# First half of the output weights: from one block at a border to side work of the attention

## The chip, the cores and the metric

One core of one Trainium2 chip runs the whole program. The metric is the device time of one execution in microseconds (us). The engines are named as in the profile: PE (TensorE, matmuls; PEld is its weight load), DVE (VectorE), ACT (ScalarE), POOL (GpSimd) and SP (SyncE, which here only issues transfers). Each engine takes its instructions in the order in which they were written into its queue, and an instruction that has to wait holds up all behind it on that engine. That holds for SP and POOL too when they issue DMAs.

## The reference, cut to what matters

An encoder layer over 2304 tokens (2048 of one sequence, 256 of another), width 1024. The change lies in how one operand of the second line is brought in:

```
n = rms_norm(x) ; [u|q|k|v] = n @ w_in
mix = concat(rms_norm(S5(u)) * ssm_out_g, rms_norm(dilated_attention(q,k,v)) * attn_out_g)
x   = x + mix @ w_out                       # w_out is 1024 x 1024
x   = x + (silu(g) * up) @ w_down , [g|up] = conv3(rms_norm(x) @ w_up)
```

Rows 0 to 511 of `w_out` multiply the S5 half of `mix` (the "a" half of the weights), rows 512 to 1023 the attention half (the "b" half). All of it is float32, and every product is made of three matmuls of split operands: each operand is a rounded part (hi) and the rest (lo), and hi\*hi + hi\*lo + lo\*hi is summed.

## The kernel before

The program runs in stages: input projection, S5 with the q/k projection, attention (with the GLU of the S5 half beside it), output projection with the second norm, up projection with the convolution, down projection. This document is about the attention and the start of the output projection.

**The attention** (from L1062 on) goes over 8 heads, two to a pair `hp`. A head has three patterns and a part for the short sequence, in 21 groups. A group is a chain over three engines: matmuls into `s` (L967, L968), a DVE reduction with the bias `bt` into `sb` (L973), an exponential on ACT (L974), transposes on PE into `pt` (L153), a copy of `pt` to `pb` (L957 on ACT or L958 on DVE; in pair 0 all on DVE), and matmuls with the values `v` into `po` (L1005, L1134). Each head has one small transpose into `pts` after its first pattern and one product `pop` near its end; both serve here as marks. At a head's second pattern POOL issues the loads of the next head's `qs`, `kh` and `kl` (L939), and SP loads the values `v` of the next pair when the old ones are free (L914 to L927). `weights` and `join` mix the three patterns of a head: SP stores and fetches small factors (`w_d`, `wb`), POOL multiplies `ot` by them, and the result goes to `ob_d`.

**Side work** fills PE beside the heads. `side_work` (L1057) says at which of the groups one step of a generator is taken. In pair 0 that is `glu`. From head 2 on it is `project_all` (L881), the projection of the S5 half: for each of 16 token tiles it loads `pat` and `pxt`, splits `pat` into `pah` (hi on ACT, L867; lo on POOL, L868), makes 24 matmuls into `ppa` (L156 to L158, 128x512) and adds the result to `pxt` on DVE (L879). A tile takes 4 steps. 48 of 120 groups take one, that is 8 a head and 12 tiles in all; the 4 tiles left are drained after the last head, before the two "early" tiles of the short sequence, whose matmuls also write `ppa`.

**The weights** are brought in by `out_weight` (L851), 8 pieces of 128x512: a load on SP (L163) into `wsoa` or `wsob`, hi on ACT (L168, into `ohia` or `ohib`) and lo on DVE (L169, into `oloa` or `olob`). The a half is called at the border between pair 0 and pair 1 (L1176), all 8 pieces in a row, with one staging buffer, since the pool `woa` has one buffer of each name. The b half is called after the attention, with two.

**What sets the order.** The lines above are not the order in the queues. A scheduler that comes with the language simulates the program and writes each engine's queue, taking earlier written work first among what it thinks is ready. So the loads of the a half, written at the border after head 1, stand in the queues from the end of the GLU on, inside head 0.

Of the kernel before, what the change touches and what calls it, by code (L numbers as in the profile page):

```python
# [10 lines left out]
F32 = mybir.dt.float32  # L11
# [3 lines left out]
AF = mybir.ActivationFunctionType  # L15
ALU = mybir.AluOpType
# [4 lines left out]
P = 128  # L21
# [51 lines left out]
def tile_encoder(ctx: ExitStack, tc: tile.TileContext, x_prompt, x_sample, norm_mix_g, w_in,  # L73
# [3 lines left out]
    nc = tc.nc  # L77
    V = nc.vector
    A = nc.scalar
# [3 lines left out]
    def mkpool(name, bufs, space=None, side=None):  # L83
        kw = {}
        if space is not None:
            kw["space"] = space
        if side is not None:
            kw["side"] = side
        return tc.tile_pool(name=name, bufs=bufs, reuse_waits="tile", **kw)
# [71 lines left out]
    def split_weight(wpool, spool, src, k0, c0, w, g, hi, lo, nm):  # L161
        s = spool.tile([P, w], F32, name="ws" + nm, tag="wstage")
        ld = nc.sync.dma_start(out=s, in_=src[k0:k0 + P, c0:c0 + w])  # L163
        if g is None:
            A.activation(hi, s, AF.Copy)
            V.tensor_tensor(lo, s, hi.bitcast(F32), ALU.subtract)
        else:
            A.activation(hi, s, AF.Copy, scale=g)  # L168
            V.scalar_tensor_tensor(lo, s, g, hi.bitcast(F32), ALU.mult, ALU.subtract)  # L169
        return ld  # L170
# [342 lines left out]
    def drain(gen, n=None):  # L513
        k = 0
        for _ in gen:
            k += 1
            if n is not None and k >= n:
                return
# [329 lines left out]
    GROUPS = [[16, 17, 0, 1, 2, 3], list(range(4, 10)), list(range(10, 16))]  # L848
    NLATE = 2

    def out_weight(wp, wst, k0, nm):  # L851
        hi = wp.tile([P, 4, D], F32R, name="ohi" + nm)
        lo = wp.tile([P, 4, D], F32R, name="olo" + nm)
        for k in range(4):
            for h in range(2):
                hs_ = slice(h * 512, (h + 1) * 512)
                split_weight(wp, wst, w_out[0], (k0 + k) * P, h * 512, 512, gains[:, 8 + k0 + k:9 + k0 + k],
                             hi[:, k, hs_], lo[:, k, hs_], f"o{nm}{k}{h}")
        return hi, lo

    def project_a(t, w, ap_, xt, psm, tag, behind=(None,)):

# [7 lines left out]
        for h in range(2):  # L870
# [7 lines left out]
                    yield  # L878
            V.scalar_tensor_tensor(xt[:, hs_], ps, rab[:, t:t + 1], xt[:, hs_], ALU.mult, ALU.add)  # L879

    def project_all(w, ap_, xp, psm):  # L881
        for t in TOKS[NLATE:]:
            xt = xp.tile([P, D], F32, name=f"pxt{t}", tag="xt")
            yield from project_a(t, w, ap_, xt, psm, "g", last_copy)
            nc.sync.dma_start(out=x1_d[t * P:(t + 1) * P, :], in_=xt)
            yield
# [62 lines left out]
    with pa:  # L949
# [107 lines left out]
        def side_work(hp, n):  # L1057

            if hp == 0:
                return n % 6 == 0  # L1060
            n -= 40
            return n * 48 // 120 != (n + 1) * 48 // 120  # L1062

        for hp in range(4):
            cs = slice(hp * P, (hp + 1) * P)
# [105 lines left out]
            if hp == 0:  # L1171
                drain(gen)
                pg.close()
                woa = right.enter_context(mkpool(name="woa", bufs=1, side="right"))
                apa = right.enter_context(mkpool(name="apa", bufs=2, side="right"))
                wa = out_weight(woa, woa, 0, "a")  # L1176
                gen = project_all(wa, apa, right.enter_context(mkpool(name="xpa", bufs=2, side="right")), ps_g)


    pu = ctx.enter_context(ExitStack())  # L1180
# [3 lines left out]
    wsum = pu.enter_context(mkpool(name="wsum", bufs=3))  # L1184
    pd = ctx.enter_context(ExitStack())
    wp = pd.enter_context(mkpool(name="wo", bufs=1))
    wst = pd.enter_context(mkpool(name="wsto", bufs=2))
    ap_ = pd.enter_context(mkpool(name="apd", bufs=2))
    xp = pd.enter_context(mkpool(name="xpd", bufs=3))
    sm = pd.enter_context(mkpool(name="smd", bufs=3))  # L1190
# [60 lines left out]
            downw[divmod(e + i, KF)] = hl[:, :, i]  # L1251

    downw = {}
    ohi, olo = out_weight(wp, wst, 4, "b")
    drain(gen)
    pgs.close()
    psm = pu.enter_context(mkpool(name="psmD", bufs=4, space=PSUM))
    pst = pu.enter_context(mkpool(name="pstD", bufs=3, space=PSUM))
# [252 lines left out]
```

## Time and profile before

| | |
|---|---|
| median of 3 runs | 2878.91 us (2878.47 to 2884.9) |
| the profiled execution | 2880.48 us, its span 2878.7 us |
| busy share of the span | PE 95%, PEld 85%, DVE 65%, ACT 46%, POOL 22% |
| mean granted TensorE clock | 0.974 |
| attention, from the first `pts` to the last `pop` | 711.4 to 1159.7 us |
| splits of the a half on ACT | 8, from 717.8 to 807.1 us |
| splits of the b half on ACT | 8, from 1163.1 to 1200.3 us |

The table is read from the page and from the views of single tiles. The busy shares are means over stages that differ; what a change in one stage is worth is read in that stage. The granted clock is 1.0 at 2.4 GHz and 0.5 at 1.2 GHz, so a stretch with 0.9 spent a fifth of its time at the lower level.

### The profile page before, as it was taken

To read this page: it belongs to the slowest core of one execution; us is meant where nothing else is said; L and a number is where in the kernel's file an instruction comes from. 1 tells how busy PE (TensorE), PEld (TensorE's weight loads), DVE (VectorE), ACT (ScalarE), POOL (GpSimd) and SP (SyncE) were. 2 spreads that over 40 slices of the span, in tenths; PEclk is the share of its full clock that TensorE was granted. 3 is DMA by queue.
4 is the path that set the end of the run, shared out by engine and by line. 5 is a ranking of instruction groups with operands and counts; after the bars stand their busy time and mean duration, and the time that the engine had idled before them with its cause. 6 is when DMAs were issued, how large, how long until landed. Compare 5 with 4: busy or idle time off the path is not lost. (4 is left out here: it accounts for less than half of the span.)

```text
span 2878.7 us, 43567 instructions
## 1 busy us (share of the span) xinstructions
PE 2744.7 (95%) x15488; PEld 2458.3 (85%) x15488; DVE 1860.5 (65%) x4274; ACT 1322.6 (46%) x2723; POOL 646.9 (22%) x1120
## 2 busy tenths in 40 slices
PE   7998889998989999888999999999999989999999
PEld 7887667788878888777999999999999978888887
DVE  5776899977745445587989997778877742223221
ACT  3354454545566666244555565556655531112110
POOL 0587533312343432220111011113100000000000
PEclk9999999999999999999999999999999999999999
DMA  7574888777788685657555555544544462224221
GB/s 215 167 249 130 252 229 233 197 188 173 148 174 193 155 195 125 227 177 228 170 174 174 192 188 156 156 156 136 167 152 152 131 182 86 74 85 142 86 84 47
DMA packets 483991, 471.04 MB, mean 164 GB/s; under 512 B 87985, under 2 KB 406077, under 8 KB 480701
## 3 DMA queue, kind: packets, MB, share of 16 engines
q1 hardware_dynamic: 465084, 425.25, 50.2%
q0 software_dynamic: 18688, 43.01, 6.4%
q8 instruction: 122, 2.00, 0.3%
q14 instruction: 97, 0.79, 0.1%
HBM read 308.63 MB, written 159.55 MB: 163 GB/s over the span
## 5 line engine op out<-in xcount | busy, mean ns | idle before, releaser
L156 PE MATMUL pf<-dw,ah 128*128 128x512 f32 x792 | 309.6, 392 | 4.9 <-ACT dw L1194 4.9
L157 PE MATMUL pf<-dw,ah 128*128 128x512 f32 x792 | 309.7, 392 | 1.7 <-DVE dw L1195 1.7
L158 PE MATMUL pf<-dw,ah 128*128 128x512 f32 x792 | 309.3, 391 | 0.0
L1479 DVE TENSOR_TENSOR acc<-pf,acc 128x512 f32<-128x512 f32 x72 | 49.7, 691 | 383.0 <-PE pf L158 383.0
L1465 ACT ACTIVATE ah<-at 128x512 fp32r<-128x512 f32 x72 | 53.1, 784 | 410.4 <-PE pf L158 410.4
L974 ACT ACTIVATE sb<-sb,st 128x256 f32<-128x256 f32 (+2 forms) x384 | 172.4, 451 | 32.9 <-DVE st L973 29.0
L1194 ACT ACTIVATE uw<-su 128x1024 fp32r<-128x1024 f32 x132 | 139.5, 1058 | 97.2 <-PE pu_5p L1378 5.6
L156 PEld LDWEIGHTS pf<-dw,ah 128*128 128x128 f32 x792 | 149.9, 189 | 37.7 <-ACT dw L1194 6.4
L157 PEld LDWEIGHTS pf<-dw,ah 128*128 128x128 f32 x792 | 149.6, 189 | 34.3 <-DVE dw L1195 3.0
L158 PEld LDWEIGHTS pf<-dw,ah 128*128 128x128 f32 x792 | 149.7, 189 | 30.7
L1195 DVE TENSOR_TENSOR uw<-su,uw 128x1024 fp32r<-128x1024 f32 x132 | 160.8, 1219 | 17.4 <-ACT uw L1194 17.3
L1422 POOL COPY r<-edge 128x2 f32<-128x2 f32 x88 | 58.3, 663 | 481.6 <-DVE h L1433 465.2
L1430 DVE SCALAR_TENSOR_TENSOR h<-r,convp,h 128x255 f32<-128x255 f32 (+3 forms) x176 | 139.8, 815 | 38.8 <-ACT h L1427 37.7
L1427 ACT ACTIVATE h<-r,convp 128x767 f32<-128x767 f32 (+2 forms) x132 | 135.5, 1028 | 63.8 <-DVE r L1414 61.2
L967 PE MATMUL s<-kh,qs 128*128 128x256 f32 (+2 forms) x384 | 151.4, 403 | 1.0 <-DVE dn L973 0.7
L1424 POOL COPY edge<-r 128x2 f32<-128x2 f32 x88 | 68.9, 783 | 368.3 <-DVE r L1414 232.6
L958 DVE COPY pb<-pt 64x128 f32<-64x128 f32 (+2 forms) x150 | 74.3, 505 | 108.1 <-PE pt L153 107.5
L1433 DVE SCALAR_TENSOR_TENSOR h<-r,convp,h 128x768 f32<-128x768 f32 (+2 forms) x176 | 140.7, 814 | 1.4
L968 PE MATMUL s<-kl,qs 128*128 128x256 f32 (+2 forms) x384 | 138.0, 369 | 0.0
L973 DVE CUSTOM_DVE_ANT_0 sb<-s,bt 128x256 f32<-128x256 f32 (+2 forms) x384 | 121.0, 357 | 13.9 <-PE pt L153 11.6
L500 POOL TENSOR_TENSOR q<-ph,phs 128x64 f32<-128x64 f32 (+6 forms) x352 | 119.4, 374 | 2.1
L153 PE MATMUL pt<-ctab,sb 128*128 128x128 f32 (+1 forms) x640 | 103.2, 284 | 8.2 <-ACT sb L974 5.9
(934 smaller groups left out, 7648.2 us busy)
## 6 DMA issues: line engine op xcount, KB each, us to landing
us<-in_w_up_dram SPq DMA_DIRECT2D x88, 512.0 KB
su<-ws_d SPq DMA_DIRECT2D x88, 512.0 KB
at<-act_d SPq DMA_DIRECT2D x36, 704.0 KB
ws_d<-su SPq DMA_DIRECT2D x44, 512.0 KB
qk_d<-qt SPq DMA_DIRECT2D x72, 256.0 KB
wb<-w_d SPq DMA_DIRECT2D x32, 384.0 KB
us<-in_w_up_dram SPq DMA_DIRECT2D x44, 256.0 KB
ds<-in_w_down_dram SPq DMA_DIRECT2D x44, 256.0 KB
```

What stands on the lines that cost most here:

```text
L156: mm = T.matmul(ps, lhi, rhi, start=first, stop=False)
L157: T.matmul(ps, lhi, rlo, start=False, stop=False)
L158: T.matmul(ps, llo, rhi, start=False, stop=last)
L967: T.matmul(ps[:, c:c + n], qs[:, q], khi[:, keys], start=True, stop=False)
L968: T.matmul(ps[:, c:c + n], qs[:, q], klo[:, keys], start=False, stop=True)
L973: V.tensor_tensor_reduce(sb[:, c:c + n], ps[:, c:c + n], bias, 1.0, 3e38, ALU.add, ALU.min, mn)
L974: A.activation(sb[:, c:c + n], sb[:, c:c + n], AF.Exp, bias=mn, scale=-1.0, accum_out=den)
L1194: A.activation(dst[:, 0], src, AF.Copy)
L1195: V.tensor_tensor(dst[:, 1], src, dst[:, 0].bitcast(F32), ALU.subtract)
L1427: A.activation(h[:, a:b], r[:, a:b], AF.Identity, bias=cw[:, 3], scale=cw[:, 1])
L1430: V.scalar_tensor_tensor(h[:, c0:c1], r[:, c0 - 1:c1 - 1], cw[:, 0], h[:, c0:c1], ALU.mult, ALU.add)
L1433: V.scalar_tensor_tensor(h[:, c0:c1], r[:, c0 + 1:c1 + 1], cw[:, 2], h[:, c0:c1], ALU.mult, ALU.add)
```

## The change

The a half becomes the first part of the generator `project_all`: three pieces are loaded ahead, and each step loads one more and splits one. It has a pool of its own, `wsa`, with four staging buffers. The b half uses the same code with four buffers in place of two, and is drained at once where it stood. Side steps are 55 of 120 groups in place of 48, of which the first 8 go to the weights.

```diff
-    def out_weight(wp, wst, k0, nm):
+    def out_weight(wp, wst, k0, nm, out):
         hi = wp.tile([P, 4, D], F32R, name="ohi" + nm)
         lo = wp.tile([P, 4, D], F32R, name="olo" + nm)
-        for k in range(4):
-            for h in range(2):
-                hs_ = slice(h * 512, (h + 1) * 512)
-                split_weight(wp, wst, w_out[0], (k0 + k) * P, h * 512, 512, gains[:, 8 + k0 + k:9 + k0 + k],
-                             hi[:, k, hs_], lo[:, k, hs_], f"o{nm}{k}{h}")
-        return hi, lo
+        def load(i):
+            k, c = divmod(i, 2)
+            t = wst.tile([P, 512], F32, name=f"wso{nm}{i}", tag="wstage")
+            nc.sync.dma_start(out=t, in_=w_out[0, (k0 + k) * P:(k0 + k + 1) * P, c * 512:(c + 1) * 512])
+            return t
+        stage = [load(i) for i in range(3)]
+        for i in range(8):
+            if i + 3 < 8:
+                stage.append(load(i + 3))
+            yield
+            k, c = divmod(i, 2)
+            cs, g = slice(c * 512, (c + 1) * 512), gains[:, 8 + k0 + k:9 + k0 + k]
+            A.activation(hi[:, k, cs], stage[i], AF.Copy, scale=g)
+            V.scalar_tensor_tensor(lo[:, k, cs], stage[i], g, hi[:, k, cs].bitcast(F32), ALU.mult, ALU.subtract)
+        out.append((hi, lo))
...
     def project_all(w, ap_, xp, psm):
+        yield from out_weight(*w, 0, "a", outw)
+        w = outw[0]
         for t in TOKS[NLATE:]:
...
-            return n * 48 // 120 != (n + 1) * 48 // 120
+            return n * 55 // 120 != (n + 1) * 55 // 120
...
-                wa = out_weight(woa, woa, 0, "a")
-                gen = project_all(wa, apa, right.enter_context(mkpool(name="xpa", bufs=2, side="right")), ps_g)
+                wsa = right.enter_context(mkpool(name="wsa", bufs=4, side="right"))
+                gen = project_all((woa, wsa), apa, right.enter_context(mkpool(name="xpa", bufs=2, side="right")), ps_g)
...
-    wst = pd.enter_context(mkpool(name="wsto", bufs=2))
+    wst = pd.enter_context(mkpool(name="wsto", bufs=4))
...
-    ohi, olo = out_weight(wp, wst, 4, "b")
+    drain(out_weight(wp, wst, 4, "b", outw))
+    ohi, olo = outw[1]
     drain(gen)
+    wa = outw[0]
```

The orders of the two programs are the same up to head 0's `pts` and again from the first products of the up projection on. Line numbers of the changed program differ: its load is L859, its hi L869, its lo L870; lines behind stand 12 to 18 higher.

**SP, from the end of the GLU to the values of pair 1.** Before, in head 0 (`at_d` is the last store of the GLU; `st_d`, `r`, `w_d` and `wb` belong to the mix of head 0):

```order
L1152 DMA st_d_120<-s_8404 32x128
L833 DMA at_d<-ga_9084 128x4x256
L163 DMA wsoa_9671<-in_w_out_dram 128x512
L163 DMA wsoa_9675<-in_w_out_dram 128x512
L1155 DMA st_d_120<-st_8417 128x4x4 x2
L1012 DMA r_8903<-st_d_120 128x4x16
L163 DMA wsoa_9679<-in_w_out_dram 128x512
L163 DMA wsoa_9683<-in_w_out_dram 128x512
L163 DMA wsoa_9687<-in_w_out_dram 128x512
L1168 DMA ob_d<-obp_8949 64x128 x2
L1029 DMA w_d_128<-w_8906 128x3x16
L1038 DMA wb_8953<-w_d_128 64x3x512 x2
```

Now, in head 1 (the first five rows stand before too, without the pieces behind them):

```order
L1168 DMA st_d_121<-s_9242 32x128
L930 DMA v_9675<-v_d 128x15x128
L1064 DMA ob_d<-ot_8061 64x512 x2
L931 DMA v_9675<-v_d 64x128
L932 DMA v_9675<-v_d 64x128
L859 DMA wsoa_9750<-in_w_out_dram 128x512
L859 DMA wsoa_9752<-in_w_out_dram 128x512
L859 DMA wsoa_9754<-in_w_out_dram 128x512
L859 DMA wsoa_9756<-in_w_out_dram 128x512
L877 DMA pat_10207<-at_d 128x4x128
L881 DMA pxt_10206<-in_x_sample_dram 128x1024
```

Before, five pieces were issued in head 0 and the sixth just ahead of the values of pair 1; the seventh and eighth came behind. Now all eight stand behind those values, four of them at once and ahead of the first `pat`.

**ACT, in the third pattern of head 1.** Before (the seventh piece is `wsoa_9695`):

```order
L974 ACTIVATE sb_9423,st_9255<-sb_9423,st_9255 128x192
L168 ACTIVATE ohia<-wsoa_9695,gains 128x512
L974 ACTIVATE sb_9455,st_9452<-sb_9455,st_9452 128x128 x4
L974 ACTIVATE sb_9480,st_9452<-sb_9480,st_9452 128x128 x4
L974 ACTIVATE sb_9523,st_9452<-sb_9523,st_9452 128x128 x3
L867 ACTIVATE pah_9782<-pat_9780 128x512
```

Now (the first piece is `wsoa_9750`):

```order
L990 ACTIVATE sb_9423,st_9255<-sb_9423,st_9255 128x192
L990 ACTIVATE sb_9455,st_9452<-sb_9455,st_9452 128x128 x3
L869 ACTIVATE ohia<-wsoa_9750,gains 128x512
L990 ACTIVATE sb_9455,st_9452<-sb_9455,st_9452 128x128
L990 ACTIVATE sb_9480,st_9452<-sb_9480,st_9452 128x128 x4
L869 ACTIVATE ohia<-wsoa_9752,gains 128x512
L869 ACTIVATE ohia<-wsoa_9754,gains 128x512
L990 ACTIVATE sb_9523,st_9452<-sb_9523,st_9452 128x128 x4
L990 ACTIVATE sb_9548,st_9452<-sb_9548,st_9452 128x128
L1158 ACTIVATE ot_9254<-po_9359 128x2x256
L990 ACTIVATE sb_9548,st_9452<-sb_9548,st_9452 128x128 x3
L869 ACTIVATE ohia<-wsoa_9756,gains 128x512
```

In the place of one split (the seventh) four stand there (the first to the fourth), and the first `pah` comes right behind the last row. The other four splits stand in head 2, in its first pattern and behind it.

**SP, at the end of the attention.** Before, around the first pieces of the b half (`ot_14025` is the load of the first tile of the output projection, `pat_13946` that of the first early tile, `wb` the factors of the last head):

```order
L1029 DMA w_d_135<-w_13653 128x3x16
L163 DMA wsob_13758<-in_w_out_dram 128x512
L1168 DMA ob_d<-obp_13696 64x128 x2
L163 DMA wsob_13762<-in_w_out_dram 128x512
L885 DMA x_d<-pxt_13790 128x1024
L865 DMA pat_13946<-at_d 128x4x128
L1038 DMA wb_13700<-w_d_135 64x3x512 x2
L1296 DMA ot_14025<-ob_d 128x4x128
```

Now:

```order
L1054 DMA wb_13705<-w_d_135 64x3x512 x2
L877 DMA pat_13949<-at_d 128x4x128
L859 DMA wsob_13753<-in_w_out_dram 128x512
L859 DMA wsob_13755<-in_w_out_dram 128x512
L859 DMA wsob_13757<-in_w_out_dram 128x512
L859 DMA wsob_13759<-in_w_out_dram 128x512
L881 DMA pxt_13865<-in_x_sample_dram 128x1024
L877 DMA pat_13984<-at_d 128x4x128
L1314 DMA ot_14029<-ob_d 128x4x128
```

The second pair of `wb` loads, which needs the buffer that POOL's first three products free, now stands ahead of the first early `pat`; before, it stood behind the loads of both early tiles. The load of `ot` has moved behind four pieces.

**PE, the `ppa` matmuls**, counted in the two orders between the marks:

| stretch | before | now |
|---|---|---|
| head 0 `pts` to head 1 `pts` | 0 | 0 |
| head 1 to head 2 | 18 | 0 |
| head 2 to head 3 | 48 | 24 |
| head 3 to head 4 | 48 | 60 |
| heads 4, 5 and 6, each to the next | 48 | 54 |
| head 7 `pts` to its `pop` | 52 | 54 |
| from there to the output projection | 122 | 132 |

In the last stretch the first matmul of an early tile stands behind 51 others before, and behind 72 now.

## Rows read from the trace of the kernel before

**Rows 1.** Busy time by stretch: us, engines' busy us and counts, clock, DMA share, GB/s.
```profile
711.40:764.40 53.00, 51.22 (x401) 44.13 (x400) 38.91 (x163) 32.05 (x109) 12.11 (x13) 0.90 0.60 126
764.40:826.60 62.20, 53.28 (x409) 45.00 (x408) 36.90 (x157) 36.20 (x127) 23.48 (x23) 0.95 0.89 189
826.60:882.80 56.20, 54.51 (x430) 46.43 (x429) 28.67 (x135) 36.69 (x127) 29.50 (x28) 1.00 0.81 166
...
997.50:1055.30 57.80, 57.80 (x436) 49.20 (x434) 28.34 (x137) 36.50 (x129) 23.27 (x23) 0.94 0.79 196
...
1159.70:1200.20 40.50, 31.81 (x134) 25.47 (x133) 18.95 (x23) 9.85 (x16) 15.73 (x13) 0.91 0.80 258
1200.20:1335.00 134.80, 122.00 (x591) 101.78 (x592) 110.95 (x453) 62.94 (x88) 28.91 (x34) 0.94 0.58 191
```

**Rows 2.** Busy time of `ppa` alone, two stretches: us, PE, PEld, DVE, clock.
```profile
1172.00:1182.30 10.30, 5.78 (x14) 4.42 (x15) 1.41 (x2) 0.68 0.70 235
1182.30:1196.00 13.70, 13.66 (x60) 10.96 (x58) 1.40 (x2) 0.99 0.78 251
```

**Rows 3.** The tile `wsoa`: what its splits waited for (us, times).
```profile
  DMA wsoa<-in_w_out_dram: 12.1, 5
```

**Rows 4.** ACT in time, heads 0 and 1: start, us, instruction, [idle before, releaser].
```profile
717.82 0.71 ACT L168 ACTIVATE ohia<-wsoa,gains 128x512 fp32r<-128x512 f32 x1
...
734.39 0.72 ACT L168 ACTIVATE ohia<-wsoa,gains 128x512 fp32r<-128x512 f32 x1 [4.62 <-DMA wsoa<-in_w_out_dram]
...
765.12 0.72 ACT L168 ACTIVATE ohia<-wsoa,gains 128x512 fp32r<-128x512 f32 x1 [2.44 <-DMA wsoa<-in_w_out_dram]
...
786.60 0.72 ACT L168 ACTIVATE ohia<-wsoa,gains 128x512 fp32r<-128x512 f32 x1 [4.36 <-DMA wsoa<-in_w_out_dram]
...
795.95 0.63 ACT L867 ACTIVATE pah<-pat 128x512 fp32r<-128x512 f32 x1 [4.39 <-DMA pat<-at_d]
```

**Rows 5.** PE in time, heads 0 and 1: its two longest waits for ACT.
```profile
735.55 0.47 PE L153 MATMUL pt<-ctab,sb 128*128 128x128 f32 x1 [1.34 <-ACT sb L974]
...
797.01 0.48 PE L153 MATMUL pt<-ctab,sb 128*128 128x128 f32 x1 [4.60 <-ACT sb L974]
```

**Rows 6.** SP in time: when the loads were issued.
```profile
713.60 6.31 SPq L163 DMA_DIRECT2D wsoa<-in_w_out_dram  x2
...
767.16 0.38 SPq L914 DMA_DIRECT2D v<-v_d  x1
...
770.76 0.83 SPq L163 DMA_DIRECT2D wsoa<-in_w_out_dram  x1
...
773.64 0.59 SPq L865 DMA_DIRECT2D pat<-at_d  x1
```

**Rows 7.** DMA issues from 700 to 830: count, KB each, median us to landing.
```profile
kl<-qk_d POOLq DMA_DIRECT2D x4, 576.0 KB, 19.3
```

**Rows 8.** Busy time by stretch, as in rows 1: head 0's wait and the loads' stretch.
```profile
730.00:740.00 10.00, 8.66 (x57) 6.90 (x56) 5.45 (x29) 5.41 (x22) 0.00 (x0) 0.77 0.74 113
740.00:760.00 20.00, 19.56 (x184) 16.85 (x184) 18.48 (x68) 14.95 (x49) 7.04 (x6) 0.86 0.18 45
...
780.00:800.00 20.00, 15.22 (x127) 12.97 (x125) 9.15 (x47) 10.43 (x41) 7.19 (x8) 0.92 1.25 233
```

**Rows 9.** PE in time behind the last `pop`: its two waits.
```profile
1176.52 0.79 PE L156 MATMUL ppa<-ohia,pah 128*128 128x512 f32 x1 [4.62 <-ACT pah L867]
...
1200.15 0.80 PE L156 MATMUL pw<-ohib,mix 128*128 128x512 f32 x1 [4.08 <-DVE x L879]
```

**Rows 10.** ACT in time there.
```profile
1174.40 0.63 ACT L1302 ACTIVATE mix<-ot 128x512 fp32r<-128x512 f32 x1 [7.21 <-DMA ot<-ob_d]
...
1175.85 0.61 ACT L867 ACTIVATE pah<-pat 128x512 fp32r<-128x512 f32 x1
```

**Rows 11.** SP in time there.
```profile
1163.57 1.69 SPq L1038 DMA_DIRECT2D wb<-w_d  x2
1165.36 1.95 SPq L1296 DMA_DIRECT2D ot<-ob_d  x2
...
1192.64 0.43 SPq L869 DMA_DIRECT2D x<-in_x_prompt_dram  x1
```

More of the change, by code (lines that the diff above doesn't have):

```diff
@@ L879, in project_a @@
             V.scalar_tensor_tensor(xt[:, hs_], ps, rab[:, t:t + 1], xt[:, hs_], ALU.mult, ALU.add)
+    outw = []
     def project_all(w, ap_, xp, psm):
+        yield from out_weight(*w, 0, "a", outw)
+        w = outw[0]
         for t in TOKS[NLATE:]:
```

## The prediction

> **What bounds the kernel now.** I read the busy shares first, then busy time by stretch between the marks `pts`, then each engine in time where a stretch is longer than its PE work, then the issues on SP and the latency of the loads.
>
> In the attention PE is the bound wherever it has side work: a stretch with 48 `ppa` matmuls is 57.8 us long with 57.8 us of PE work [rows 1]. Side work at full clock costs 13.66 us for 60 matmuls, 0.228 us each [rows 2]; the 48 are 10.9 us, so the heads' own part of such a stretch is 57.8 - 10.9 = 46.9 us.
>
> The two stretches that the a half touches stand apart. Head 0's has 53.0 us with 51.22 of PE and clock 0.90; the next, with only 18 `ppa` matmuls, has 62.2 us with 53.28 of PE [rows 1]. Less work takes longer there. ACT shows why: its splits wait 12.1 us for `wsoa`, in 5 times [rows 3], 4.62 us in head 0, 2.44 and 4.36 in head 1, and then 4.39 more for the first `pat` [rows 4]. An exponential stands behind each, and PE waits for it 1.34 and 4.60 us [rows 5].
>
> How long a piece takes depends on what else is being loaded. The first, issued at 713.60 [rows 6], is split at 717.82 [rows 4]: 4.2 us. The seventh, issued at 770.76 behind `v`, is split at 786.60: 15.8 us. `pat`, issued at 773.64, is used at 795.95: 22.3 us. In that time POOL's loads for the next head (`kl`, 576 KB, 19.3 us to landing [rows 7]) and SP's `v` share the DMA engines: 780 to 800 us moves 233 GB/s with PE busy 15.22 of 20 us, while 740 to 760 moves 45 [rows 8]. The DMA engines lie nearly idle just where the old pieces stood, and are full where the new ones go. The Trainium skill ("DMA: Bandwidth & Descriptors", Issuing engines are not separate DMA queues) says that transfers started by SP and by GpSimd run on the same 16 DMA engines and interleave. By that rule more pieces in this stretch delay each other and `pat`; the trace agrees, 15.8 us for a piece here against 4.2 in head 0.
>
> **Part by part.** Copies and splits are as many as before (16 loads, 16 hi, 16 lo), and the `ppa` matmuls are 432 in both. What changes is where they stand.
>
> *Head 0* loses five loads, and the splits with them. What can be won is between the 1.34 us that PE waited visibly [rows 5] and the 4.62 us that ACT stood [rows 4]. But 740 to 760 us, where no piece is waited for, has PE at 19.56 of 20 us at clock 0.86, with DVE at 18.48 of 20 [rows 8]: in pair 0 DVE also makes all copies, so it stays close to the bound. I take **-2**.
>
> *The border and head 1* (the 62.2 us stretch). The wait of 2.44 at 765 us goes, since no piece stands there. The 18 `ppa` matmuls leave: 18 x 0.228 = 4.1 us. Against that, four splits stand in the third pattern where one stood. The seventh piece was issued at 770.76 and waited for until 786.60; the first new one goes out in `pat`'s old place, 773.64 [rows 6]. With the same latency of 15.8 us it lands at 789.4. ACT came to its split at 786.60 - 4.36 = 782.2 [rows 4], so it waits 7.2 us in place of 4.4, with at most five rows of exponentials in between to soften it. Three more pieces follow in SP's queue, 0.75 MB, at 233 GB/s 3.4 us; the three splits behind use that up while ACT works. `pat` comes behind them, but its `pah` is now wanted only behind four splits and at head 2, so its 4.39 us goes. What bounds this: below, both waits of the third pattern go, 2.44 + 4.36 = 6.8 us won; above, the splits wait as long as `pat` did (22.3 us from 773.64 is 795.9, 13.7 us behind 782.2) with no help from the wait that goes, 13.7 - 4.4 = 9.3, some 8 with the exponentials ahead. I take **+3** before the side work that leaves, since the seventh piece is the nearest row and half of what ACT loses reached PE before.
>
> *Side work put elsewhere.* The two stretches of heads 1 and 2 lose 18 + 24 = 42 `ppa` matmuls, 9.6 us. They come back in full in stretches that PE fills (12, 6, 6 and 6 more in heads 3 to 6, 2 in head 7, 10 behind it: 42), +9.6. The question is what heads 1 and 2 give up for it. A stretch cannot shrink under its slowest other engine: head 0's with no `ppa` is 53.0 us, not 46.9 [rows 1], and the one with 24 left would be 46.9 + 24 x 0.228 = 52.4 at best against 56.2 now, a gain of 3.8 at most, and with four splits more on ACT and DVE I take 2.4. Head 1's, 62.2 long, should give back its 4.1 in full, as PE was held up there by ACT and not by its own work. Together 6.5 given up, 9.6 paid: **+3**. Bounds: 0 where all of it shrinks, +5.5 where only head 1's 4.1 does.
>
> *The tail.* Between the last `pop` and the output projection PE is busy 31.81 of 40.5 us [rows 1]. Two waits make 8.7 us: 4.62 for the first early tile's `pah` and 4.08 for `x` [rows 9]. The first is a queue matter: ACT stands 7.21 us for `ot` at 1174.40, and `pah` follows at 1175.85 [rows 10]. Now 72 - 51 = 21 more matmuls stand ahead of that early tile, 21 x 0.228 = 4.8 us of cover, just the size of the wait. But SP is held by the second `wb`, which waits for three POOL products, and now stands ahead of `pat`, four pieces, `pxt` and `ot`; before, `wb` and `ot` were issued at 1163.57 and 1165.36 [rows 11] with `pat` already out. The 4 pieces are 1 MB, 3.9 us at that stretch's 258 GB/s [rows 1]. The last `x` was issued at 1192.64 [rows 11] and with deeper staging goes out sooner, so part of the 4.08 can go too. The clock of 0.68 behind the first wait [rows 2] rises or falls with it. Ends: -8.7 and, with both waits paid a second time, +8. I take **0**: the cover and the added queue are of a size.
>
> *The four buffers of the b half* let pieces start two earlier. The splits there end at 1200 with PE waiting for `x`, not for a piece, so nothing is won apart from the tail's term. The stages before head 0 and behind the first up products have the same order: 0.
>
> **The sum.** -2 + 3 + 3 + 0 = +4 on the profiled 2880.48: 2884.5. The median of the runs stands 1.6 below the profiled execution, so the forecast is **2883**. That the loads are "three ahead" is no gain by itself: in the queues the old pieces stood in the quiet head 0, and the new ones come later, not earlier.
>
> **The rivals.**
>
> *A, faster: the loads land before they are wanted.* Four pieces go out together ahead of the first split. If ACT reaches the first split later than the queue tells, or the first piece takes nearer 10 us than 15.8, no split waits. Then head 0 gives 2 to 4.6, the third pattern 2.44 + 4.36, the tail 4.08, less the side work's 3: -9.9 to -12.5, and up to 1.6 more with the clock of 780 to 800 (0.92 [rows 8], so 8% of 20 us lost to the lower level): -10 to -14 on the median, 2865 to 2869. For it: 780 to 800 has 4.8 us of idle PE to give. Against: the latency row. The Trainium skill ("DMA: Bandwidth & Descriptors", Rules for kernel authors) says to issue a DMA early, compute, and wait on its semaphore late; by that rule this is the outcome, if early meant the place in the queue. The trace speaks against it here, with 773.6 for the first issue in place of 713.6. Chance 0.23.
>
> *B, slower: the first piece is stuck among the loads of head 2 and the values.* Place: ACT, third pattern of head 1. The first piece takes as long as `kl` or `pat` (19.3 to 22.3 us), ACT's four splits take the exponentials behind them along, PE idles and its clock falls to the lower level for some us. Price: 9 us of wait over the old one, 3 to 5 for the pieces behind it and `pat`, 2 for the clock (1.6 were lost there before), with the side work's 3 and less head 0's 2: +15 to +17, 2894 to 2896. It decides when the first piece lands 10 us or more behind ACT's arrival. For it: DMA share 1.25 in that stretch [rows 8]. Against: POOL's loads were issued earlier and are partly through by 789. Chance 0.17.
>
> *C, slower by little: the tail loses.* SP, held by `wb`, issues the early `pat` and `ot` late; PE waits 5 us more for `pah`, with the rest as forecast: +9, 2888. It decides when the early `pat` is issued later than some 1170, since 72 matmuls (16.4 us) cover a latency of that length behind the last `pop` at 1159.7. Chance 0.13.
>
> **How the numbers follow.** The forecast has the 0.47 that are left. 0.3% of 2878.9 is 8.6 us, about what a measurement of this kernel can tell from no change. Faster by that (under 2870.3): nearly all of A, 0.22, and 0.01 of the forecast's lower tail. Slower (over 2887.5): B's 0.17, half of C, 0.06, and 0.05 of the forecast, together 0.28. Within: the rest, 0.49. The range reaches from inside A to just over B, 2866 to 2897; what is left out is the case where all of head 0's, head 1's and the tail's gains come at once, and the one where B and C do.
>
> **What would show it.** Head 0's stretch near 51 us with no wait for a piece on ACT. A wait of about 7 us on ACT ahead of the first `wsoa` split in head 1 and no long one ahead of the three behind it; none there means A, over 10 means B. `pts` marks some 61 us apart from head 1 to head 2, 54 from 2 to 3, 60.5 from 3 to 4, 59 after that. No PE wait of 4 us ahead of the early tile; one of 8 or more with a late `pat` means C. I am wrong in the mechanism if the pieces land in under 10 us in that stretch, or if heads 1 and 2 shrink by the full 9.6 us of the work that leaves them.

## The result and the profile after

The changed kernel takes 2906.47 us (median of 3, 2904.01 to 2911.17) against 2878.91: the ratio is 1.0089, 95% interval 1.0069 to 1.0108. It is slower, beyond the upper end of the forecast range (2897). Its profiled execution takes 2904.01 us with a span of 2902.2, 23.5 us over the span before.

Busy time by stretch of the changed kernel, columns as in [rows 1]; the first five stretches run from one `pts` to the next (heads 0, 1, 2, 3 and 5), the last is the tail from the last `pop` to the output projection:

```profile
709.69:759.25 49.56, 47.65 (x401) 41.30 (x399) 35.70 (x161) 30.15 (x108) 15.94 (x16) 0.97 0.51 103
759.25:818.06 58.81, 51.84 (x394) 44.61 (x393) 35.62 (x150) 38.23 (x128) 19.43 (x21) 0.85 0.87 213
818.06:889.57 71.51, 54.03 (x402) 45.59 (x401) 27.81 (x137) 35.30 (x122) 31.20 (x30) 0.83 0.55 108
889.57:952.05 62.48, 59.78 (x447) 50.83 (x446) 28.41 (x139) 38.57 (x132) 20.98 (x22) 0.97 0.87 198
...
1010.57:1074.76 64.19, 59.52 (x440) 50.76 (x439) 27.83 (x135) 37.32 (x127) 23.46 (x24) 0.95 0.79 183
...
1178.40:1221.30 42.90, 33.80 (x140) 27.01 (x134) 18.59 (x27) 10.47 (x17) 13.95 (x13) 0.88 0.90 294
```

Head 2 stands out: 71.5 us against 56.2 [rows 1], though it has half the side work. The forecast's steps beside what the two profiled executions show:

| stretch | before | after | difference | forecast |
|---|---|---|---|---|
| head 0 | 53.0 | 49.6 | -3.4 | -2 |
| head 1 | 62.1 | 58.8 | -3.3 | +3 - 4.1 = -1.1 |
| head 2 | 56.2 | 71.5 | **+15.3** | -2.4 |
| heads 3 to 6 | 230.5 | 246.4 | **+15.9** | 30 x 0.228 = +6.8 |
| head 7 and the tail | 86.8 | 85.3 | -1.5 | 12 x 0.228 + 0 = +2.7 |
| ahead of head 0, and from the output projection on | 2390.0 | 2390.6 | +0.6 | 0 |
| sum | 2878.7 | 2902.2 | +23.5 | +4 |

The forecast missed by 19.5 us: the two rows in bold are 17.7 and 9.1 us over it, the others 7.2 under it. Each stretch is of one execution. In a second profiled execution of the changed kernel (e10 below) head 2 takes 72.5 us and heads 3 to 6 together 248.2, so the two bold rows repeat. Head 0 takes 54.1 us there, at a granted clock of 0.81 in place of 0.97, so its gain does not.

**Head 2.** PE in time, all its waits of over 1 us there:

```profile
852.58 0.69 PE L153 MATMUL ptp<-ctab,sbp 128*128 128x128 f32 x2 [4.68 <-ACT sbp L993]
...
874.09 1.98 PE L1150 MATMUL po<-pb,v 128*64 128x64 f32 x32 [10.46 <-ACT ot L1161]
```

ACT, one step back from each:

```profile
852.02 0.51 ACT L993 ACTIVATE sbp<-sbp,dn 128x256 f32<-128x256 f32 x1 [6.43 <-DVE dn L992]
...
873.01 1.03 ACT L1161 ACTIVATE ot<-po 128x512 f32<-128x512 f32 x1 [9.96 <-POOL ot L1061]
```

The shorter wait goes back to DVE, which stood 6.07 us for `r` (small factors of head 2 that come back through DRAM; SP stored them only behind the wait for `w_d` that follows below):

```profile
850.96 0.74 DVE L1034 TENSOR_TENSOR mm<-r 128x16 f32<-128x16 f32 x1 [6.07 <-DMA r<-st_d]
```

The longer one ends with POOL. POOL in time, with head 3's loads first (of the six only the ends are shown), then products (L1059) and additions (L1061) of the mix:

```profile
821.90 0.59 POOL L955 DMA_DIRECT2D qs<-qk_d  x1 [19.35 <-ACT ot L1156]
...
824.78 1.07 POOL L955 DMA_DIRECT2D kl<-qk_d  x2
847.97 3.70 POOL L1059 TENSOR_TENSOR ot<-ot,wb 128x512 f32<-128x512 f32 x3 [22.13 <-DMA wb<-w_d]
...
858.68 3.78 POOL L1059 TENSOR_TENSOR ot<-ot,wb 128x512 f32<-128x512 f32 x3 [1.68 <-DMA wb<-w_d]
...
869.27 2.48 POOL L1059 TENSOR_TENSOR ot<-ot,wb 128x512 f32<-128x512 f32 x2 [3.14 <-DMA wb<-w_d]
871.71 2.49 POOL L1061 TENSOR_TENSOR ot<-ot,ot 128x512 f32<-128x512 f32 x2
```

SP in time: the store of head 1's factors `w_d` and the loads `wb` that read it back; and what SP waited for (us in total, times, longest):

```profile
823.59 0.37 SPq L1045 DMA_DIRECT2D w_d<-w  x1
...
840.63 1.31 SPq L1054 DMA_DIRECT2D wb<-w_d  x2
```

```profile
SPq L1054 <- DMA w_d<-w: 18.8, 2, 16.6
SPq L859 <- DMA v<-v_d: 16.7, 1, 16.7
```

The store of 24 KB goes out 1.7 us behind the first of POOL's six loads of 576 KB, and SP waits 16.6 us for it to land. The same rows of the kernel before, SP and then POOL:

```profile
817.63 0.36 SPq L1029 DMA_DIRECT2D w_d<-w  x1
819.92 1.30 SPq L1038 DMA_DIRECT2D wb<-w_d  x2
```

```profile
826.65 3.75 POOL L1043 TENSOR_TENSOR ot<-ot,wb 128x512 f32<-128x512 f32 x3 [22.66 <-DMA wb<-w_d]
...
831.60 1.14 POOL L939 DMA_DIRECT2D qs<-qk_d  x2
```

There the store is 14 us ahead of the loads and lands in under 2.3 us, so POOL's products start at 826.65 in place of 847.97 (each counted from head 2's `pts`: 0.1 and 29.9 us). Head 1's mix then ends late, its third `ot` (one buffer) comes free late, and PE's next group waits for it. The last row of POOL above holds a second cause, which e11 takes up: the addition that frees this `ot` stands behind two products of head 2 there (869.27), while before all of head 1's additions stood ahead of them.

What all of head 2 costs: PE idles 17.5 us in place of 1.7 (+15.8). It loses 24 matmuls (-5.5), and yet its busy time only falls from 54.51 to 54.03. The other 5.0 us go with the granted clock, 0.83 in place of 1.00 (an estimate from windows of 1 us puts what the lower level cost PE's busy time at some 6). Behind the long wait one stretch stands wholly at the lower level of 1.2 GHz:

```profile
868.00:878.00 10.00, 3.83 (x44) 3.23 (x44) 1.42 (x5) 2.76 (x4) 5.63 (x5) 0.50 0.17 43
```

**Heads 3 to 6.** Here DVE waits for `r`, the small factors of the first two patterns that come back through DRAM. DVE's waits for it from head 0 to the output projection, before and after (19.7 of the 27.3 us stand in heads 3 to 6):

```profile
DVE mm L1018 <- DMA r<-st_d: 6.6, 4, 3.3
```

```profile
DVE mm L1034 <- DMA r<-st_d: 27.3, 6, 7.0
```

PE's waits that follow from it in heads 3 and 5, and head 6's:

```profile
925.06 0.38 PE L983 MATMUL s<-kh,qs 128*128 128x256 f32 x1 [2.70 <-DVE dn L989]
...
1046.55 0.58 PE L983 MATMUL s<-kh,qs 128*128 128x256 f32 x1 [4.67 <-DVE dn L989]
...
1107.04 0.78 PE L153 MATMUL pt<-ctab,sb 128*128 128x128 f32 x4 [1.99 <-DVE pb L974]
```

Together 9.4 us, and with the 6.8 of the 30 added matmuls 16.2: the measured 15.9.

**Head 1.** The wait that the forecast looked for is there. ACT and PE in time:

```profile
787.64 0.72 ACT L869 ACTIVATE ohia<-wsoa,gains 128x512 fp32r<-128x512 f32 x1 [12.52 <-DMA wsoa<-in_w_out_dram]
```

```profile
788.80 0.48 PE L153 MATMUL pt<-ctab,sb 128*128 128x128 f32 x1 [5.40 <-ACT sb L990]
```

One wait of 12.52 us for the first piece stands in the place of those of 4.36 and 4.39 [rows 4], and PE's is 5.40 in place of 4.60 [rows 5].

**The tail.** PE's two waits of [rows 9] are gone, and two others stand there, of 5.88 and 3.22 us. The first, what ended it on DVE, and the issue of the first early tile's `pat` on SP:

```profile
1192.95 0.77 PE L156 MATMUL ppa<-ohia,pah 128*128 128x512 f32 x1 [5.88 <-DVE pxt L891]
```

```profile
1192.05 1.41 DVE L891 SCALAR_TENSOR_TENSOR pxt<-ppa,rab,pxt 128x512 f32<-128x512 f32 x2 [9.63 <-DMA pxt<-in_x_sample_dram]
```

```profile
1189.72 0.55 SPq L877 DMA_DIRECT2D pat<-at_d  x1
```

The `pxt` that DVE waited for belongs to a side tile, not to an early one. PE then takes the first early tile 72 matmuls behind the last `pop`, without a wait.

### The profile page after: what moved, and what is told of

Same layout as the page of the kernel before. It is cut to its first block, busy times and chain, and to the rows that moved or that the text cites. A ratio compares the mean times of both kernels' runs of the same rounds, so it can differ in the third digit from the quotient of the medians.

```text
span 2902.2 us, 43582 instructions
## 1 busy us (share of the span) xinstructions
PE 2741.1 (94%) x15488; PEld 2454.1 (85%) x15488; DVE 1855.3 (64%) x4274; ACT 1326.9 (46%) x2723; POOL 648.6 (22%) x1120
## 5 line engine op out<-in xcount | busy, mean ns | idle before, releaser
L990 ACT ACTIVATE sb<-sb,st 128x256 f32<-128x256 f32 (+2 forms) x384 | 172.7, 452 | 50.0 <-DVE st L989 43.6
L1211 DVE TENSOR_TENSOR uw<-su,uw 128x1024 fp32r<-128x1024 f32 x132 | 160.9, 1220 | 17.6 <-ACT uw L1210 17.5
L1440 POOL COPY r<-edge 128x2 f32<-128x2 f32 x88 | 58.5, 664 | 480.9 <-DVE h L1451 472.1
L983 PEld LDWEIGHTS s<-kh,qs 128*128 128x128 f32 x384 | 106.8, 278 | 13.3 <-DVE dn L989 8.7
```

Of the source, the lines that this page charges most:

```text
L983: T.matmul(ps[:, c:c + n], qs[:, q], khi[:, keys], start=True, stop=False)
L990: A.activation(sb[:, c:c + n], sb[:, c:c + n], AF.Exp, bias=mn, scale=-1.0, accum_out=den)
L1211: V.tensor_tensor(dst[:, 1], src, dst[:, 0].bitcast(F32), ALU.subtract)
```

## The experiments

Theory S: in head 2 the store of head 1's small factors meets the storm of head 3's loads. Theory D: from head 3 on DVE reaches `mm` ahead of `r`. Rival R: head 2 is slow because late pieces, splits and thin side work stand in it. The kernel before ran beside each group, and each ratio is against it. "Attention and tail" runs from head 0's `pts` to the first product of the output projection (`pw`). The three columns on the right are of the profiled execution.

| run | median us | ratio (95%) | head 2, us | `w_d` to `wb`, us | attention and tail, us |
|---|---|---|---|---|---|
| before | 2878.91 | | 56.2 | 2.3 | 488.7 |
| changed | 2906.47 | 1.0089 (1.0069 to 1.0108) | 71.5 | 17.0 | 511.6 |
| e10, changed again | 2913.9 | 1.0120 (1.0091 to 1.0148) | 72.5 | 17.8 | 518.5 |
| e1 | 2895.0 | 1.0043 (1.0030 to 1.0057) | 65.6 | 1.7 | 511.2 |
| e2 | 2893.83 | 1.0052 (1.0031 to 1.0073) | 73.6 | 15.5 | 502.9 |
| e3 | 2891.87 | 1.0041 (1.0024 to 1.0059) | 63.5 | 1.7 | 499.6 |
| e4 | 2904.0 | 1.0076 (1.0058 to 1.0094) | 72.2 | 16.7 | 506.7 |
| e5 | 2892.62 | 1.0044 (1.0028 to 1.0061) | 62.9 | 1.7 | 504.7 |
| e6 | 2900.04 | 1.0068 (1.0043 to 1.0093) | 73.1 | 17.7 | 510.5 |
| e7 | 2893.48 | 1.0048 (1.0034 to 1.0062) | 62.5 | 1.7 | 496.7 |
| e8 | 2881.66 | 1.0003 (0.9990 to 1.0017) | 57.1 | 2.8 | 488.4 |
| e9 | 2891.14 | 1.0035 (1.0023 to 1.0047) | 65.2 | 1.7 | 498.1 |
| e11 | 2908.0 | 1.0098 (1.0081 to 1.0115) | 66.9 | 17.6 | 512.2 |

The medians of e1, e5 and e6 hold a gain that does not come from the attention. From the first `pw` to the end, their profiled executions take 1668.5 to 1672.3 us, those of all other runs 1677.0 to 1682.4. In the changed kernel PE waits 5.9 us for DVE ahead of the products `pu_1p` of the up projection; in e1 it waits 2.4 there, for another tile:

```profile
PE pu_1p L1396 <- DVE r213y L148: 5.9, 1, 5.9
```

```profile
PE pu_1p L1398 <- DVE uw L1213: 2.4, 1, 2.4
```

None of the edits was aimed at that place. So the argument below rests on the waits and the stretches, and on the last column, more than on the medians.

**e10: the changed kernel again.** 

> The changed kernel itself, unchanged, on the chip of this call: how far its stretches repeat. S: w_d to wb 15-19 us in head 2, PE's wait for ot 9-12 us, head 2's stretch 70-74, in all 2902-2911. If head 2's length were chance of one execution, it would lie elsewhere.

Head 2 repeats: PE waits 9.54 us for `ot` and 6.86 for `ptp` there. The total, 2913.9 us, lies 2.9 over the range that was named; the ratio on that chip is 1.0120.

**e1: the loads behind the products.**

```diff
-head_q[nx // 2, nx % 2] = load_head(nx // 2, nx % 2, done)[0]
+head_q[nx // 2, nx % 2] = load_head(nx // 2, nx % 2, prod[hd - 1, 0] if hd == 2 else done)[0]
```

> The changed kernel, in which the loads of head 3 on POOL wait for POOL's first three products of head 1, as they stand in the kernel before; nothing else moves. Theory S (the small factors of head 1 are stored into a storm: head 3's loads go out 2 us before the store of w_d, which then takes 17 us in place of 2 until wb can be issued; the products, ot's buffers and PE follow): w_d to wb back to under 4 us, PE's wait of 10.5 us for ot gone, head 2's stretch from 71.5 to 54-58 us, in all 2888-2894 us. Rival R (head 2 is slow because the last four splits and the thin side work stand in it and the clock falls): stretch 67-72, in all 2903-2909. Rival Q (POOL is merely held 3 us by issuing the loads): 3-4 us gained, 2900-2903.

The store lands at once, both waits of head 2 are gone, and head 2 is 5.9 us shorter. Rival Q falls: 15.1 us of waits go together with the store's round trip, not 3. Not all is as expected: head 2 is 65.6 us, between the 54 to 58 of S and the 67 to 72 of R, the total is 1.0 us over S's range, and the attention and tail take as long as in the changed kernel. The ratio of 1.0043 therefore owes most to the place behind the attention. SP, and PE's waits of over 1 us in head 2:

```profile
831.95 0.37 SPq L1045 DMA_DIRECT2D w_d<-w  x1
833.63 1.31 SPq L1054 DMA_DIRECT2D wb<-w_d  x2
```

```profile
864.08 0.98 PE L983 MATMUL s<-kh,qs 128*128 128x192 f32 x3 [3.38 <-DMA kh<-qk_d]
...
869.32 0.50 PE L984 MATMUL s<-kl,qs 128*128 128x192 f32 x1 [4.26 <-DMA kl<-qk_d]
```

Now head 3's loads are late (issued from 846.4 us on), which costs 7.6 us in place of the 15.1. In this run POOL's last addition of head 1 also stands ahead of head 2's products again, so e1 takes away both causes at once.

**e2: the kernel before with the same lateness.**

```diff
-                weights(hd, *sts)
+                store = weights(hd, *sts)
+                if hd != 1:
+                    store()
...
+                        if hd == 2:
+                            wait_for(late[1](), first_ld[0])
+                            join(1, late[0])
```

> The kernel before, in which the store of head 1's factors w_d waits until the first load of head 3's qs has landed, so that POOL has those loads ahead of the products, as in the changed kernel; weights and side work as before. S: the same chain appears without the change: POOL's products start some 20 us later (about 847 us in place of 827), ACT waits 6-11 us for ot in head 2's last pattern and PE with it, head 2's stretch 56 -> 64-72, in all 2887-2895. R: head 2 stays at 56-58, in all 2877-2882.

Head 2 grows from 56.2 to 73.6 us, without any of the change, with the same wait:

```profile
836.45 0.36 SPq L1034 DMA_DIRECT2D w_d<-w  x1
851.95 1.29 SPq L1045 DMA_DIRECT2D wb<-w_d  x2
```

```profile
885.67 1.98 PE L1144 MATMUL po<-pb,v 128*64 128x64 f32 x32 [10.03 <-ACT ot L1155]
```

R falls as the whole cause: here the pieces and the 48 `ppa` matmuls stand as before. The effect is larger than named (64 to 72), and the products start at 859.75 us, not at 847. POOL's last addition of head 1 stands behind head 2's products here too, so e2 brings in both causes at once.

**e5: the loads behind the store alone.**

```diff
-head_q[nx // 2, nx % 2] = load_head(nx // 2, nx % 2, done)[0]
+head_q[nx // 2, nx % 2] = load_head(nx // 2, nx % 2, stored[hd - 1] if hd in (2,) else done)[0]
```

> The changed kernel, in which the loads of head 3 on POOL wait only until head 1's store of w_d has landed, not for the products as in e1. The storm then starts behind that store, and some 15 us earlier than in e1 (there POOL issued them at 846 us, and PE waited 7.7 us for kh and kl). S: w_d to wb under 4 us, the 10.5 us for ot gone or under 3, the waits for kh and kl gone; head 2's stretch 56-61 us (71.5 in the changed kernel, 65.6 in e1); in all 2887-2894 us. R (what was left in e1's head 2 is the splits and the thin side work): head 2 stays at 64-67, in all 2894-2900.

`w_d` to `wb` is 1.7 us and the wait for `ot` falls from 10.46 to 2.14. Head 2 is 62.9, between the two expectations: 2.92 us for `kl` are left, 2.44 for DVE and 1.17 more. The store's wait is cured, the storm itself is not. POOL's last addition of head 1 stands ahead of head 2's products in this run too.

**e11: POOL's last addition of head 1 ahead of head 2's first products.** In the changed order the addition that frees the third `ot` had moved behind head 2's products, which wait for their own `wb`. POOL's order in the changed kernel, and in e11:

```
ot_8979<-ot_8979,ot_9254    (head 1)        ot_8979<-ot_8979,ot_9254
ot_9702<-ot_9702,wb_10312   (head 2)        ot_8979<-ot_8979,ot_9451
ot_9910<-ot_9910,wb_10312   (head 2)        ot_9702<-ot_9702,wb_10312
ot_8979<-ot_8979,ot_9451    (head 1, last)  ot_9910<-ot_9910,wb_10312
```

> The changed kernel, in which POOL's last addition of head 1 (which frees the one buffer of the third ot) stands ahead of the first products of head 2, as in the kernel before, and not behind them; head 3's loads stay ahead of head 1's store of w_d. It divides PE's 10.5 us in two. By the rows of the changed kernel the addition could run at 866 in place of 872.9, when head 1's other work on POOL is done. S with this second cause: w_d to wb still 15-19 us, the wait of 4.7 us for ptp stays, the wait for ot falls from 10.5 to 2-5 us, head 2's stretch from 71.5-72.5 to 64-68; in all 6-8 us less than the changed kernel (2906 on one chip, 2914 on another): 2898-2907. If the storm alone sets it, the wait stays at 9-11 and head 2 at 70-74. If the order alone does, the wait goes to 0 and ptp's too, head 2 at 56-60.

The waits and head 2 (66.9 us) come out as named for both causes; the total, 2908.0, lies 1.0 over its range. PE in time:

```profile
859.01 0.69 PE L158 MATMUL ptp<-ctab,sbp 128*128 128x128 f32 x2 [7.30 <-ACT sbp L998]
...
874.66 1.98 PE L1159 MATMUL po<-pb,v 128*64 128x64 f32 x32 [4.23 <-ACT ot L1170]
```

With the order on POOL mended and the store still behind the loads, 4.23 of the 10.46 us are left, and head 2 is 4.6 us shorter than in the changed kernel (5.6 than in e10). With the store ahead of the loads as well (e5), 2.14 are left, the wait for `ptp` is gone, and head 2 is another 4.0 us shorter. So both causes are shown, each with the other left as it was. The total does not show the first: the attention and tail take 512.2 us, against 511.6 and 518.5 in the two executions of the changed kernel, and the intervals of the ratios overlap.

**e6: `mm` of heads 3 to 6 later on DVE.**

```diff
-                weights(hd, *sts)
+                if hd not in (3, 4, 5, 6):
+                    weights(hd, *sts)
...
+                if hd in (3, 4, 5, 6):
+                    weights(hd, *sts, behind=last_copy[0])
```

> The changed kernel, in which DVE takes the first step of the weights (mm, which waits for r) of heads 3 to 6 only behind the copy pbp of that head, an order on DVE alone. Theory D (in the changed order mm stands ahead of or between the reductions of the last group, r is not there, DVE stands 27.3 us over the program against 6.6 before, and PE with it in heads 3, 5 and 6: 2.7, 4.7 and 2.0 us): DVE's waits for r under 12 us, those three PE waits gone, heads 3, 5 and 6 from 62.5, 64.2 and 61.2 to about 60, 59.5 and 59; in all 2895-2900. Rival (these heads are long by their 54 to 60 ppa matmuls alone): nothing gained, 2902-2908; and if the later store of w_d meets the next head's loads, another head gets longer by 5-15 us instead.

DVE's waits for `r` fall from 27.3 to 10.4 us, and in heads 3 to 6 from 19.7 to none. Heads 3, 5 and 6 are 58.0, 59.2 and 59.8 us long with no PE wait for DVE left: D is shown for these waits. Head 4 takes the gain back, 58.5 -> 65.3 (though it took 64.1 in e10 as well, where PE waits for DVE). The factors `w_d` of the head before go out 9.9 us ahead of its `pts` in place of 22.2, so the six products that stand ahead of its POOL loads start later, the loads of `qs`, `kh` and `kl` are issued 14.9 us behind `pts` in place of 5.5, and PE waits:

```profile
PE s L989 <- DMA kl<-qk_d: 5.0, 1, 5.0
```

**e3 and e9: the a half as a block again.** e3 drains the a half at the border, with 48 steps; e9 adds the cures of e5 and, for head 3, of e6.

```diff
-                gen = project_all((woa, wsa), apa, ...
+                drain(out_weight(woa, wsa, 0, "a", outw))
+                gen = project_all(outw[0], apa, ...
```

> The changed kernel, but the a half is drained at the border in one block (through the new loads, three ahead, four buffers) and side steps are 48 of 120 as before; the ppa matmuls stand as in the kernel before (18, 48, 48 ...). Its pieces go out ahead of pair 1's values again, and four splits stand in head 0. On POOL the loads of head 3 stand ahead of the products of head 1. S, if the order on POOL is what counts: head 2's stretch still 62-70 us, in all 2883-2893. S, if only the time of w_d against the loads counts: w_d goes out before them and head 2 stays at 56-58; with 5-8 us won in heads 0 and 1, 2869-2874. R: head 2 at 56-58, heads 0 and 1 as in the changed kernel or better, 2869-2874.

> The kernel of e3 (a half in one block at the border, three ahead, four buffers) with two of the cures: head 3's loads behind the store of w_d (e5), and head 3's mm behind pbp (e6), since DVE stood 11.3 us over r there and PE 8.1. S and D: head 3 from 65.1 to 57-58, head 2 from 63.5 to 59-62; in all 2891.9 - 10 = 2880-2885, level with the kernel before, and under it only if heads 0 and 1 keep their 2.4 us. Rival (a later store of head 3's w_d meets the next loads, as in e6's head 4): another head gets 5-8 us longer, 2886-2892.

In e3 `w_d` goes out 3.5 us ahead of the loads and its round trip is short, though the loads stand ahead of the products on POOL: for the round trip the time of the store against the loads counts, not the order of the products. But head 2 keeps 63.5 us and the total is 2891.87, as was named for the case that the order on POOL counts. PE's only wait of over 1 us in head 2 is 1.90 us for DVE, and its busy time is 59.2 us in place of 54.5 at a clock of 0.95; why is not shown. In head 3 DVE and PE stand, in this order:

```profile
937.94 0.17 DVE L1032 TENSOR_TENSOR mm<-r 128x16 f32<-128x16 f32 x1 [11.33 <-DMA r<-st_d]
```

```profile
939.36 0.79 PE L156 MATMUL ppa<-ohia,pah 128*128 128x512 f32 x1 [8.13 <-DVE pb L972]
```

e9 removes that (head 3 from 65.1 to 58.1) and loses it elsewhere: heads 2, 4 and 5 are 1.7, 2.2 and 2.6 us longer. Its median is 0.7 us under e3's. The total is the one that its rival named, but no single head is 5 to 8 us longer, and what lengthens these three was not tried.

**e4: the loads at the border.** One line, `drain(gen, 1)`, behind the generator's creation.

> The changed kernel, but the generator's first step (the four loads) is taken at the border, so that the four pieces are issued ahead of pair 1's values; the splits stay side work, 55 of 120. All theories: ACT's 12.5 us wait for the first piece goes, PE's 5.4 with it; head 1 from 58.8 to 52-55. S: the loads of head 3 still stand ahead of head 1's products and of w_d, so head 2 stays at 66-72; in all 2898-2903. R (late pieces and their splits are the cause of head 2's length too): head 2 falls to 54-58 as well, in all 2882-2888.

The first piece is now split with a wait of 2.14 us, but ACT waits 11.4 us for four pieces in place of 12.5 for one, and PE 4.7 in place of 5.4. Head 1 is 57.4 us, above the 52 to 55 that every theory named; head 2 stays at 72.2, and the total is 1.0 us over S's range. The forecast weighed, in the Trainium skill ("DMA: Bandwidth & Descriptors", Rules for kernel authors), the advice to issue a DMA early and wait late. Here the earlier issue alone brought 1.4 us in its stretch. That is within what single executions differ by: head 1 takes 59.8 us in e10, and 60.0 in e7, which issues early too, against 59.8 in e5, which does not.

**e7: all three (e4, e5, e6).** 

> The changed kernel with all three: the four loads issued at the border (e4), head 3's loads behind the store of w_d (e5), mm of heads 3 to 6 behind pbp (e6). If S and D are the whole cause, the gains add up: 2906 - 14 - 8 - 3 = 2881, with 2876-2886 as the span, the kernel before again within noise. If something else is lost in the change: 2888-2896.

About half comes back (ratio 1.0048 in place of 1.0089), not all, as was named for the case that something else is lost. The attention and tail take 496.7 us: 14.9 of the 22.9 us that the change had cost there are back, more than in e5, and 8.0 are not. The median is level with e5's all the same, since e7 lacks e5's gain behind the attention. The five waits named by S and D are gone or under 3 us; head 6 takes 7.4 for `kh` and `kl`, as head 4 took 5.0 for `kl` in e6.

**e8: four buffers for the b half alone.** 

> The kernel before with four staging buffers in place of two for the b half, and nothing else. All theories: the attention as before (the order is the same up to head 7), the tail within 2 us; 2876-2883 us. More than 4 us either way would mean that the b half has a part of its own in the result.

No effect; the b half has no part in the result. No version that ran is faster than the kernel before.

## Why the prediction was wrong

**The step that failed** is "Side work put elsewhere", where head 2 was to shrink "under its slowest other engine" by 2.4 us. It grew by 15.3. The sum took a stretch to be as long as the work of its busiest engine and looked for waits in the attention only where pieces and `pat` are loaded. It put those at nothing that lie on the way of `w`, `w_d`, `wb` and `ot`: it did not follow these past the head that they belong to, nor POOL's order, where head 3's loads had moved ahead of head 1's six products. The prediction's own rows held the warning: `kl` takes 19.3 us to land [rows 7], and the store of `w_d` goes out at the same time as the next such loads. What stood in its place is two waits of PE, 4.68 us for `ptp` and 10.46 for `ot`, and a clock of 0.83. e2 makes the chain in the kernel before, e1 and e5 take its waits away, e11 shows POOL's part alone, and e5 against e11 the part of the store. That the missing 18 matmuls let head 2's first pattern overtake head 1's factors is argued from the marks (`w_d` 9 us ahead of head 2's `pts` before, 5.5 behind it now) and was not tried by itself; e3, with the 18 back, has `w_d` ahead of the loads again. Neither of the two signs that the prediction named for a wrong mechanism came up (the first piece took 19.7 us, and heads 1 and 2 grew by 12.0 us together): both look at the pieces and the work, not at the mix.

The same step failed for heads 3 to 6. Their +6.8 us of side work was right, but the changed orders put `mm` ahead of the last group's reductions on DVE, and 9.4 us of waits for `r` came on top (e6).

**Right, point by point.** Head 0: -3.4 against -2, inside the bounds of 1.3 to 4.6, but not in e10 (54.1 us); in e1, e4 to e7 and e11 it takes 49.6 to 51.6. Head 1: the mechanism was right, ACT's wait mis-sized, 12.5 us in place of 7.2. The first piece took 19.7 us from its issue to its split (767.93 to 787.6), not 15.8, and ACT came to it 15.9 us behind head 1's `pts`, not 17.8. It cost PE less than feared, and head 1 shrank by 3.3 in place of 1.1. The tail: "0" was near by luck. Both waits of [rows 9] are replaced by two of 5.88 and 3.22 us, but for `pxt`, which the prediction had not weighed; with 2.7 us more work the stretch from head 7 is 1.5 shorter. The b half: nothing, as said (e8).

**The rivals.** B ended on the right side with the wrong place. It held the first piece 13 us behind ACT's arrival, which came true almost to the number (12.5), and priced it at +15 to +17; but that wait alone left head 1 shorter than before. The storm of head 3's loads, a head later, made the time. C's condition came true and its price did not: the first early `pat` was issued 11.7 us behind the last `pop`, behind the second `wb` as C said, where C asked for some 10.3. But PE had by then stood for `pxt`, the early `pah` was there in time, and PE's two waits sum to 9.1 us against 8.7. A fell: the pieces did not land before they were wanted, not even when issued earlier (e4).

**A reading of the prediction.** Its 46.9 us for a head's own part come from a stretch at clock 0.94 [rows 1], so the 52.4 us "at best" for head 2 were no bound: the kernel before, at clock 1.00, has 54.5 - 10.9 = 43.6 us of PE work there without the side work. The miss does not come from this.

**Open.** In e1, e3, e5, e7 and e9 head 2 stays at 62.5 to 65.6 us, where the forecast's count gives 53.8 and the kernel before, with 48 matmuls as in e3 and e9, has 56.2. PE idles 4.3 to 10.1 us there in place of 1.7, and the granted clock is 0.79 (e1) to 0.95 in place of 1.00. The waits that are left are for `kh` and `kl`, DVE and ACT, and which of them would remain with all factors in time was not tried.

## What to carry to other kernels

When side work is moved, the heads beside it run at another pace, and whatever was in step by chance falls out of it. Look for the small transfers that make a round trip through DRAM (store, wait, load) and ask which large loads will be under way when they go out; a 24 KB store then took 17 us in place of 2. Compare the order of every engine that has both loads and work in its queue, not only those that the change names.

## What the runs showed that was not expected

From the issue of a 24 KB store to the load that waits for it took 15.5 to 17.8 us in the six executions in which it went out 1.7 to 5.3 us behind the first of six loads of 576 KB, and 1.7 to 2.8 us in the seven in which it went out ahead of them. The Trainium skill ("DMA: Bandwidth & Descriptors", Issuing engines are not separate DMA queues) says that transfers from different engines interleave on the same 16 DMA engines; the trace agrees, and shows what that cost the small one here.

SP held the fourth piece back for 16.7 us until a load of `v` had landed, which shares no data with it and stands ahead of it in SP's queue. Why is not shown by a run. `pat` behind it went out at 786.54 us, 18.6 behind the first piece.

A cure of one wait was answered by another four times (e1, e6, e7, e9): each shift in time found a new wait, most often for a transfer of the next head.
